# One Square for both token tiles of the q projection, and other places for sink copies, reciprocals and weight splits, in a hybrid decoder step

## The chip, the cores and the metric

The kernel runs on one core of a Trainium2 chip. TensorE (PE) multiplies and transposes, VectorE (DVE), ScalarE (ACT) and GpSimd (POOL) do the rest, and SyncE (SP) issues DMAs. The metric is the device time of the whole program in microseconds, the median of several runs. The times and the profile of the kernel before were shown ahead of the prediction; of the changed kernel its code and the order of its instructions, and no time.

## What is computed

One layer of a decoder, for a prompt of 2048 tokens and for 8 sample tokens. Inputs are normalised and modulated, one projection gives q, k, v and the gates, and two branches follow: sliding-window attention with normalised q and k and a sink in the softmax, and a gated linear recurrence. Gated projections merge both.

```
h = _rmsnorm(x, norm_g) * (1.0 + scale) + shift
z = h @ w_in
q, k, v, ga, xr, gr, ma, mr = jnp.split(z, offs, axis=-1)
q = _rmsnorm(q.reshape(B, T, N_HEADS, HEAD_DIM), q_g)
k = _rmsnorm(k.reshape(B, T, KV_HEADS, HEAD_DIM), k_g)
...
logits = jnp.einsum('bnqkgd,bnskd->bnkgqs', qb, kb) * ATT_SCALE
logits = jnp.where(valid, logits + _rel_bias(rel_table, dist), NEG)
p = softmax(concatenate([logits, sinks]))[..., :-1]
o = jnp.einsum('bnkgqs,bnskd->bnqkgd', p, vb)
ya = o * jax.nn.silu(ga)
...
merged = jax.nn.sigmoid(ma) * (ya @ w_pa) + jax.nn.sigmoid(mr) * (yr @ w_pr)
y = x + gate * (merged @ w_out)
```

D_MODEL is 1024, with 16 query heads and 4 key heads of 64, and a window of 128. The change lies in the prompt's attention, where q is projected and normalised.

## The kernel before, in words

All matrix products of float32 data are made of three: each operand is split into a high and a low part (`split_raw`: ACT copies the high part, DVE subtracts it from the raw data for the low part), and high x high, high x low and low x high are summed in PSUM. Weights arrive raw by DMA in tiles of 128x512 and are split on the chip; one such split is one CAST on ACT and one TENSOR_TENSOR on DVE.

The prompt is worked in two halves of 1024 tokens (s = 0, 1). Each half has an attention pass (`phase_attn`), which in the profile takes about 108 to 340 us and 1035 to 1258 us, and a long run of projections after it (`line`).

An attention pass loops over i = 0 to N + 1, with N = 16. Iteration i stands for q group u = i // 4 (four heads, 256 columns of w_in) and token block tp = i % 4 (two tiles t = 0, 1 of 128 tokens). It is a software pipeline of three steps: iteration i projects and normalises q of step i, does the scores and the softmax of step i-1, and the products with v of step i-2. The stages, by the names of the code:

- `gemm_a`, twice ("half 0" and "half 1", one for each token tile): 24 matmuls of 128x256 into columns 0:256 and 256:512 of one PSUM bank, `pg`. In the profile these are the rows `MATMUL pg<-B,S 128x256`.
- `stage_a1(ps, ss, t)` for each half: ACT squares the half (`ACTIVATE H<-pg 128x256`), DVE sums the squares of each head (`TENSOR_REDUCE M<-H 128x4`), and POOL takes mean, epsilon and the power -1/2 (`rstd_of`: `TENSOR_SCALAR M<-M`, `TENSOR_TENSOR M<-M,mhalf`).
- `stage_a2`: DVE multiplies q by that factor, once for each tile (`TENSOR_TENSOR B<-pg,M 128x256`).
- `stage_b1` of step i-1: PE transposes q (four matmuls `pt<-ident,B`, between half 0 and half 1), ACT and DVE make its high and low part (`ACTIVATE B<-pt,qg`, `SCALAR_TENSOR_TENSOR B<-pt,qg,B`).
- `stage_b2`: the scores, 64-row matmuls into `pq`, `pg` and `pt`. `stage_b0`: POOL copies the sinks into the last column of the softmax tile (`COPY B<-skn 128x4`). `stage_b3`, once for each tile: DVE masks and adds the bias (`COPY_PREDICATED`, then a custom reduction, named ISA in the order), ACT takes four exps.
- `stage_b4` of step i-2: DVE's RECIPROCAL of the sums, and POOL's product with it (`TENSOR_TENSOR B<-B,M 128x512`), once for each tile.
- `stage_c1` of step i-2: eight transposes of the softmax tiles (four for each tile), then "parts": for each tile an ACT copy (`COPY B<-pt`) and a DVE product with a mask (`TENSOR_TENSOR B<-pt,mcT`). `stage_c2`: 16 matmuls with v. `stage_c3` takes them out.
- `fill`: a gate projection's matmuls, in the first and last iterations; `slot(n)`: pieces of the following projections, in i = 13 to 16; in the second pass also the sample's own steps (`stage_s`, `samples_gemm`), small matmuls of 8 rows and their norm, in the iterations with tp > 0.
- `weights(n, end)`: takes the splits that are due, by a list of (place, end) pairs. The q weights of u = 1, 2, 3 are four splits each, due at places 3 to 6, 11 to 14 and 19 to 22, where place 2i stands for the first part of iteration i and 2i + 1 for its later part, and end = 0 or 1 for two spots in each. The last gate weights (called gKT here) are due at 31.

Every instruction of the pass goes through the wrapper `Pinned` (line 60 in all rows of the profile), which keeps program order: each engine runs its instructions in the order in which they are written, and waits at the first one that is not ready. So the order of the calls in the loop is the order on every engine. Tiles come from rings: `B` (`Tt`, 35 tiles of 128x512) and `H` (6 of 128x256).

Of the kernel before, what the change touches and what calls it, by code (L numbers as in the profile page):

```python
# [26 lines left out]
HD = 64  # L27
# [14 lines left out]
def tile_hybrid_step(ctx: ExitStack, tc: tile.TileContext, x_prompt, x_sample, cache_k, cache_v, state_conv,  # L42
# [63 lines left out]
    def H(shape, dt=F32):  # L106
        return hp.tile([P] + shape, dt, tag="H", name=nm("H"))
# [132 lines left out]
    def rstd_of(dst, ss, n, inv):  # L240
        G_.tensor_scalar(dst, ss, inv, EPS, op0=ALU.mult, op1=ALU.add)
        G_.tensor_tensor(dst, dst, mhalf[0:dst.shape[0], 0:n], op=ALU.pow)
# [315 lines left out]
    def phase_attn(s, hT, sa, kT, vt, chunks, line):  # L558

        ya, mbs, kcs = {}, {}, {}  # L560

        def stage_a1(ps, ss, t):
            sq = H([256])
            A.activation(sq, ps[:, t * 256:(t + 1) * 256], AF.Square)
            o = ss[:, 4 * t:4 * t + 4]
            V.tensor_reduce(o, sq.rearrange("p (h d) -> p h d", d=HD), op=ALU.add, axis=AX.X)
            rstd_of(o, o, 4, 1.0 / HD)

        def stage_a2(ps, ss):
            qn = Tt([2, 2, 2, HD])  # L570
# [243 lines left out]
        for i in range(N + 2):  # L814
            gsm_ready = len(gsm)

            def fill(n):
                nonlocal hdone
                while hdone < n:
                    evac = ga_half(hdone)  # L820
                    if evac:
                        evac()
                    hdone += 1

            def slot(n):
                if N - 3 <= i <= N:
                    line.emit(4 * (i - N - 1) + n)

            if 2 <= i:
                lt_[i - 2] = [stage_b4(*sm_[i - 2][0])]  # L830
            weights(2 * i, 0)
            if 2 <= i:
                lt_[i - 2].append(stage_b4(*sm_.pop(i - 2)[1]))
            if 1 <= i <= N:
                ub, tb = seq[i - 1]
                if tb == 0 and ub % 2 == 0:
                    mbs[ub // 2] = S([8, P])
                    ld.dma_start(mbs[ub // 2], Md[:, ub // 2 * 8:ub // 2 * 8 + 8])
            slot(0)
            if i < N:  # L840
                u, tp = seq[i]
                ps_[i], ss_[i] = PG(), M([8])
                gemm_a(ps_[i], wqs[u], hT, 2 * tp * P, 0)
                stage_a1(ps_[i], ss_[i], 0)
            elif i == N:
                fill(nh - 3)
            else:
                line.emit(0)
            if 1 <= i <= N:
                qk_[i - 1] = stage_b1(ub, tb, qn_.pop(i - 1))  # L850
            weights(2 * i, 1)
            slot(1)
            if i < N:
                if s == 1 and tp == 1:
                    next(smp[u])
                if pend:
                    next(pend.pop(0))
                gemm_a(ps_[i], wqs[u], hT, (2 * tp + 1) * P, 1)
                if pend:
                    next(pend.pop(0))  # L860
                if tp == 3:
                    drop(wqs.pop(u))
                if s == 1 and tp == 1:
                    next(smp[u])
                stage_a1(ps_[i], ss_[i], 1)
            elif i == N:
                fill(nh - 2)
            else:
                line.emit(1)
            weights(2 * i + 1, 0)  # L870
            if 2 <= i:
                t2 = seq[i - 2][1]
                c_[i - 2] = [stage_c1(2 * t2 + t, lt) for t, lt in enumerate(lt_.pop(i - 2))]
                c_[i - 2] = [fn() for fn in c_[i - 2]]
            slot(2)
            if i == N + 1:
                line.emit(2)
            if 1 <= i <= N:
                lps = stage_b2(ub, tb, *qk_.pop(i - 1))
                lts = [stage_b0(ub) for _ in range(2)]  # L880
            if 2 <= i:
                u2, t2 = seq[i - 2]
                po = stage_c2(u2, c_.pop(i - 2))
                if u2 == 3:
                    free(vt[1][t2])
            if 1 <= i <= N:
                sm_[i - 1] = [stage_b3(ub, 2 * tb, lps[0], lts[0])]
            if i < N:
                qn_[i] = stage_a2(ps_.pop(i), ss_.pop(i))
            if 2 <= i and u2 > 0:  # L890
                stage_c3(u2, t2, po)
            if 1 <= i <= N:
                sm_[i - 1].append(stage_b3(ub, 2 * tb + 1, lps[1], lts[1]))
                if ub % 2 and tb == 3:
                    free(mbs.pop(ub // 2), *kT[ub // 2])
            fill(want[i] if i < N else nh)
            if 2 <= i and u2 == 0:
                stage_c3(u2, t2, po)
            if 2 <= i and t2 == 3:
                for f in (2 * u2, 2 * u2 + 1):  # L900
                    st.dma_start(yad[s, f], ya[f])
                    free(ya.pop(f))
            weights(2 * i + 1, 1)
            if s == 1 and i < N and tp > 0:
                next(smp[u])
            if gsm and gsm_ready:
                next(gsm.pop(0))
            slot(3)
# [1236 lines left out]
```

## Time and profile before

| what | value |
| --- | --- |
| runs before, median | 1985.59 us (1983.94 to 1988.86, three runs) |
| the profiled execution | 1991.77 us, its span from first to last instruction 1990.1 us |
| mean granted clock of TensorE | 0.995 |
| busy PE, DVE, ACT, POOL | 97%, 69%, 50%, 21% of the span |
| instructions | 32504 |

A line of the costliest groups gives engine, operation, out<-in by the names of tiles, shape, count, then busy us in all and mean ns of one, then the idle time of the engine just ahead of these instructions and what ended most of it. A line of the timeline gives start in us from the span's start, duration in us, engine and operation, how many alike were merged, and in brackets the idle time ahead and its releaser. A row of the windows gives the stretch and its length, then the busy time of PE, of its weight loads (PEld), DVE, ACT and POOL, the granted clock (1.00 is full), and the share and GB/s of the DMA engines. A row of the waits reads: who waited <- for whom: us in all, times, longest.

### The profile page before, as it was taken

How to read it: one execution, taken by the hardware profiler on the slowest of the kernel's cores; microseconds unless marked ns; L12 is line 12 of the kernel's file. 1: busy time of each engine (PE TensorE's matmuls, PEld its weight loads, DVE VectorE, ACT ScalarE, POOL GpSimd, SP SyncE). 2: the span in 40 equal slices, each digit the busy share in tenths (PEclk: the TensorE clock that was granted, in tenths of full speed). 3: DMA queues.
4: the chain of work that ended last, by engine and by line, in shares of the span. 5: the costliest groups of instructions: out<-in, count | busy, mean ns of one | idle time of the engine just before them, and what ended most of it. 6: DMA issues, size and time to landing. Idle time of an engine off the chain costs nothing. (4 is left out here: it accounts for less than half of the span.)

```text
span 1990.1 us, 32504 instructions
## 1 busy us (share of the span) xinstructions
PE 1930.7 (97%) x11504; PEld 1571.9 (79%) x11504; DVE 1375.0 (69%) x2894; ACT 988.4 (50%) x2199; POOL 409.4 (21%) x540
## 2 busy tenths in 40 slices
PE   6899999999999999999999999999999999999999
PEld 4788887778888878887898888777887877777777
DVE  3447777766878885578744766677677879754965
ACT  4335555435665766514423555543465757542221
POOL 4113443000201112152012344310011111111600
PEclk9999999999999999999999999999999999999999
DMA  9520214552433457986622121445233334458673
GB/s 304 178 75 12 86 49 148 151 183 87 150 98 113 143 180 226 321 296 191 224 60 57 36 62 49 143 130 153 78 118 100 127 102 164 141 174 291 219 230 111
DMA packets 307688, 286.62 MB, mean 144 GB/s; under 512 B 57073, under 2 KB 224229, under 8 KB 307486
## 3 DMA queue, kind: packets, MB, share of 16 engines
q1 hardware_dynamic: 307398, 282.41, 45.3%
q8 instruction: 90, 1.47, 0.3%
q0 software_dynamic: 128, 2.15, 0.3%
q14 instruction: 72, 0.59, 0.1%
HBM read 200.69 MB, written 85.93 MB: 144 GB/s over the span
## 5 line engine op out<-in xcount | busy, mean ns | idle before, releaser
L60 PE MATMUL pg<-S,B 128*128 128x512 f32 (+1 forms) x4224 | 1003.8, 392 | 4.2 <-DVE B L60 3.8
L60 PEld LDWEIGHTS pg<-S,B 128*128 128x128 f32 (+1 forms) x4224 | 773.5, 188 | 189.5 <-issue 11.9
L60 DVE TENSOR_TENSOR B<-B,B 128x512 fp32r<-128x512 f32 (+1 forms) x732 | 537.8, 757 | 157.7 <-ACT B L60 147.9
L60 PE MATMUL pq<-S,B 128*128 128x512 f32 (+2 forms) x1920 | 411.0, 378 | 5.9 <-DVE B L60 5.7
L60 PEld LDWEIGHTS pq<-S,B 128*128 128x128 f32 (+1 forms) x1920 | 316.3, 187 | 84.1 <-DVE B L60 9.7
L60 POOL TENSOR_TENSOR B<-B,B 128x512 f32<-128x512 f32 x128 | 191.3, 1511 | 926.3 <-DVE B L60 518.3
L60 ACT CAST B<-B 128x512 fp32r<-128x512 f32 x468 | 280.3, 617 | 111.2 <-DVE B L60 72.1
L60 PE MATMUL pg<-B,S 128*128 128x256 f32 x1872 | 249.0, 289 | 17.6 <-ACT H L60 12.8
L60 PEld LDWEIGHTS pg<-B,S 128*128 128x128 f32 x1872 | 231.9, 192 | 36.6 <-ACT H L60 19.8
L60 ACT CAST S<-B 128x512 fp32r<-128x512 f32 x184 | 108.8, 620 | 95.8 <-DVE B L60 40.3
L60 DVE TENSOR_TENSOR S<-B,S 128x512 fp32r<-128x512 f32 x184 | 143.2, 808 | 14.8 <-ACT S L60 14.6
L60 ACT ACTIVATE B<-B 128x512 f32<-128x512 f32 (+1 forms) x150 | 93.1, 630 | 116.4 <-DVE B L60 108.7
L60 ACT ACTIVATE B<-B,M 128x129 f32<-128x129 f32 x260 | 102.6, 396 | 72.1 <-DVE M L60 53.4
L60 POOL TENSOR_TENSOR B<-B,M 128x512 f32<-128x512 f32 x64 | 70.4, 1121 | 170.4 <-DVE M L60 170.4
L60 DVE SCALAR_TENSOR_TENSOR B<-B,pg 128x512 f32<-128x512 f32 x78 | 53.1, 682 | 74.8 <-PE pg L60 67.0
L60 POOL TENSOR_TENSOR M<-M,mhalf 128x4 f32<-128x4 f32 (+3 forms) x102 | 96.3, 944 | 8.5
L60 DVE TENSOR_TENSOR B<-pq,B 128x512 f32<-128x512 f32 x96 | 65.9, 686 | 44.1 <-PE pq L60 37.9
L60 ACT COPY B<-pg 128x512 f32<-128x512 f32 x80 | 46.9, 586 | 90.1 <-PE pg L60 81.7
L60 DVE TENSOR_REDUCE M<-H 128x4 f32<-128x256 f32 (+1 forms) x85 | 35.1, 414 | 80.3 <-ACT H L60 79.0
L60 ACT COPY H<-pt 128x256 f32<-128x256 f32 (+1 forms) x47 | 15.6, 333 | 150.1 <-PE pt L60 150.1
L60 DVE SCALAR_TENSOR_TENSOR B<-B,VT,B 128x512 f32<-128x512 f32 x96 | 81.1, 845 | 2.3
L60 DVE SCALAR_TENSOR_TENSOR B<-B,B 128x512 f32<-128x512 f32 x106 | 72.0, 684 | 0.4 <-ACT B L60 0.2
(201 smaller groups left out, 1711.5 us busy)
## 6 DMA issues: line engine op xcount, KB each, us to landing
B<-in_w_in_dram SPq DMA_DIRECT2D x144, 256.0 KB
B<-in_w_in_dram SPq DMA_DIRECT2D x128, 128.0 KB
B<-yad SPq DMA_DIRECT2D x56, 256.0 KB
B<-hd SPq DMA_DIRECT2D x48, 256.0 KB
B<-in_w_out_dram SPq DMA_DIRECT2D x48, 256.0 KB
S<-in_w_ada_dram SPq DMA_DIRECT2D x32, 256.0 KB
S<-in_x_prompt_dram SPq DMA_DIRECT2D x16, 512.0 KB
hd<-B SPq DMA_DIRECT2D x32, 256.0 KB
```

Of the source, the lines that this page charges most:

```text
L60: ins = fn(*args, **kw)
```

## The change

`stage_a1` now squares the whole bank with one ACT instruction, after half 1, into a tile of the `B` ring. The reduction and the factor are a stage of their own, `stage_a3`: one TENSOR_REDUCE to 128x8 and one eight-wide `rstd_of`, behind the parts of c1. The sinks' copies of `stage_b0` stand ahead of these parts. `weights` is called once in an iteration, between the transposes of b1 and half 1. `slot(2)` stands behind c2. The two `stage_b4` are written as one list.

```diff
@@ -559,12 +559,17 @@
 
         ya, mbs, kcs = {}, {}, {}
 
-        def stage_a1(ps, ss, t):
-            sq = H([256])
-            A.activation(sq, ps[:, t * 256:(t + 1) * 256], AF.Square)
-            o = ss[:, 4 * t:4 * t + 4]
-            V.tensor_reduce(o, sq.rearrange("p (h d) -> p h d", d=HD), op=ALU.add, axis=AX.X)
-            rstd_of(o, o, 4, 1.0 / HD)
+        def stage_a1(ps):
+            sq = Tt([512])
+            A.activation(sq, ps, AF.Square)
+            return sq
+
+        def stage_a3(sq):
+            ss = M([8])
+            V.tensor_reduce(ss, sq.rearrange("p (h d) -> p h d", d=HD), op=ALU.add, axis=AX.X)
+            free(sq)
+            rstd_of(ss, ss, 8, 1.0 / HD)
+            return ss
 
         def stage_a2(ps, ss):
             qn = Tt([2, 2, 2, HD])
@@ -827,10 +832,7 @@
                     line.emit(4 * (i - N - 1) + n)
 
             if 2 <= i:
-                lt_[i - 2] = [stage_b4(*sm_[i - 2][0])]
-            weights(2 * i, 0)
-            if 2 <= i:
-                lt_[i - 2].append(stage_b4(*sm_.pop(i - 2)[1]))
+                lt_[i - 2] = [stage_b4(*x) for x in sm_.pop(i - 2)]
             if 1 <= i <= N:
                 ub, tb = seq[i - 1]
                 if tb == 0 and ub % 2 == 0:
@@ -839,16 +841,15 @@
             slot(0)
             if i < N:
                 u, tp = seq[i]
-                ps_[i], ss_[i] = PG(), M([8])
+                ps_[i] = PG()
                 gemm_a(ps_[i], wqs[u], hT, 2 * tp * P, 0)
-                stage_a1(ps_[i], ss_[i], 0)
             elif i == N:
                 fill(nh - 3)
             else:
                 line.emit(0)
             if 1 <= i <= N:
                 qk_[i - 1] = stage_b1(ub, tb, qn_.pop(i - 1))
-            weights(2 * i, 1)
+            weights(2 * i + 1, 1)
             slot(1)
             if i < N:
                 if s == 1 and tp == 1:
@@ -862,27 +863,30 @@
                     drop(wqs.pop(u))
                 if s == 1 and tp == 1:
                     next(smp[u])
-                stage_a1(ps_[i], ss_[i], 1)
+                sq = stage_a1(ps_[i])
             elif i == N:
                 fill(nh - 2)
             else:
                 line.emit(1)
-            weights(2 * i + 1, 0)
             if 2 <= i:
                 t2 = seq[i - 2][1]
                 c_[i - 2] = [stage_c1(2 * t2 + t, lt) for t, lt in enumerate(lt_.pop(i - 2))]
+            if 1 <= i <= N:
+                lts = [stage_b0(ub) for _ in range(2)]
+            if 2 <= i:
                 c_[i - 2] = [fn() for fn in c_[i - 2]]
-            slot(2)
+            if i < N:
+                ss_[i] = stage_a3(sq)
             if i == N + 1:
                 line.emit(2)
             if 1 <= i <= N:
                 lps = stage_b2(ub, tb, *qk_.pop(i - 1))
-                lts = [stage_b0(ub) for _ in range(2)]
             if 2 <= i:
                 u2, t2 = seq[i - 2]
                 po = stage_c2(u2, c_.pop(i - 2))
                 if u2 == 3:
                     free(vt[1][t2])
+            slot(2)
             if 1 <= i <= N:
                 sm_[i - 1] = [stage_b3(ub, 2 * tb, lps[0], lts[0])]
             if i < N:
@@ -900,7 +904,6 @@
                 for f in (2 * u2, 2 * u2 + 1):
                     st.dma_start(yad[s, f], ya[f])
                     free(ya.pop(f))
-            weights(2 * i + 1, 1)
             if s == 1 and i < N and tp > 0:
                 next(smp[u])
             if gsm and gsm_ready:
```

Three places show how the order of instructions moves. The first is on PE, iteration i=6 of the first pass, at the step from half 0 over the transposes of b1 to half 1 (`pg_2417` before and `pg_2387` now are the projection's bank, `pt_...` the transposes' bank). Before:

```order
L60 MATMUL pg_2417<-B_1959,S_869 128x256
L60 MATMUL pg_2417<-B_1958,S_869 128x256
L60 MATMUL pt_2448<-ident_81,B_2390 128x128 [waits DVE_49,PE_49]
L60 MATMUL pt_2448<-ident_81,B_2390 128x128
L60 MATMUL pt_2448<-ident_81,B_2390 128x128 [waits DVE_49]
L60 MATMUL pt_2448<-ident_81,B_2390 128x128
L60 MATMUL pg_2417<-B_1711,S_337 128x256 [waits Activation_49]
L60 MATMUL pg_2417<-B_1712,S_337 128x256
```

and now:

```order
L60 MATMUL pg_2387<-B_1938,S_869 128x256
L60 MATMUL pg_2387<-B_1937,S_869 128x256
L60 MATMUL pt_2412<-ident_81,B_2364 128x128 [waits DVE_49,PE_49]
L60 MATMUL pt_2412<-ident_81,B_2364 128x128
L60 MATMUL pt_2412<-ident_81,B_2364 128x128 [waits DVE_49]
L60 MATMUL pt_2412<-ident_81,B_2364 128x128
L60 MATMUL pg_2387<-B_1583,S_337 128x256
L60 MATMUL pg_2387<-B_1584,S_337 128x256
```

The same instructions stand in the same order; the first matmul of half 1 no longer waits for ACT.

The second place is on ACT in the same iteration, from the last exps of the iteration ahead to the first copy of c1's parts (CAST is the split's part; `pt_2448` and `pt_2412` are b1's transposes, `pt_2501` and `pt_2466` those of c1). Before:

```order
L60 ACTIVATE B_2367,M_2400<-B_2367,M_2393 128x129 [waits DVE_49] x3
L60 CAST B_2409<-B_1763 128x512 [waits DMAHW1_49,DMAHW0_49,Activation_49]
L60 ACTIVATE H_2443<-pg_2417 128x256 [waits PE_49]
L60 ACTIVATE B_2453<-pt_2448,qg_944 128x512 [waits PE_49]
L60 CAST B_2457<-B_1766 128x512 [waits DMAHW3_49,DMAHW2_49]
L60 ACTIVATE H_2491<-pg_2417 128x256 [waits PE_49]
L60 COPY B_2509<-pt_2501 128x512 [waits PE_49,Activation_49]
```

and now:

```order
L60 ACTIVATE B_2301,M_2374<-B_2301,M_2367 128x129 [waits DVE_49] x3
L60 ACTIVATE B_2417<-pt_2412,qg_944 128x512 [waits PE_49,Activation_49]
L60 CAST B_2421<-B_1750 128x512 [waits DMAHW3_49,DMAHW2_49,Activation_49]
L60 CAST B_2431<-B_1941 128x512 [waits DMAHW5_49,DMAHW4_49,Activation_49]
L60 ACTIVATE B_2459<-pg_2387 128x512 [waits PE_49,Activation_49]
L60 COPY B_2478<-pt_2466 128x512 [waits PE_49]
```

The first half's Square is gone and the second covers 512 columns; both CASTs stand between the high part of q and that Square, where before one stood ahead of the first Square.

The third place is DVE in the same iteration, from b4's reciprocals to the first mask copy of b3 (`mcT` marks c1's products). Before:

```order
L60 TENSOR_TENSOR B_2410<-B_1763,B_2409 128x512 [waits DMAHW1_49,DMAHW0_49,Activation_49]
L60 RECIPROCAL M_2385<-M_2385 128x4
L60 RECIPROCAL M_2400<-M_2400 128x4
L60 TENSOR_REDUCE M_2418<-H_2443 128x4 [waits Activation_49]
L60 SCALAR_TENSOR_TENSOR B_2454<-pt_2448,qg_944,B_2453 128x512 [waits Activation_49]
L60 TENSOR_TENSOR B_2458<-B_1766,B_2457 128x512 [waits DMAHW3_49,DMAHW2_49,Activation_49]
L60 TENSOR_REDUCE M_2418<-H_2491 128x4 [waits Activation_49]
L60 TENSOR_TENSOR B_2506<-pt_2496,mcT_90 128x512 [waits PE_49]
L60 TENSOR_TENSOR B_2508<-pt_2501,mcT_90 128x512 [waits Activation_49]
L60 COPY_PREDICATED pq_2512<-maskf_88,pq_2512 128x2x128 [waits PE_49]
```

and now:

```order
L60 RECIPROCAL M_2359<-M_2359 128x4 [waits Activation_49]
L60 RECIPROCAL M_2374<-M_2374 128x4 [waits Activation_49]
L60 SCALAR_TENSOR_TENSOR B_2418<-pt_2412,qg_944,B_2417 128x512 [waits Activation_49]
L60 TENSOR_TENSOR B_2422<-B_1750,B_2421 128x512 [waits DMAHW3_49,DMAHW2_49,Activation_49]
L60 TENSOR_TENSOR B_2432<-B_1941,B_2431 128x512 [waits DMAHW5_49,DMAHW4_49,Activation_49]
L60 TENSOR_TENSOR B_2475<-pt_2461,mcT_90 128x512 [waits PE_49]
L60 TENSOR_TENSOR B_2477<-pt_2466,mcT_90 128x512 [waits Activation_49]
L60 TENSOR_REDUCE M_2481<-B_2459 128x8
L60 COPY_PREDICATED pq_2485<-maskf_88,pq_2485 128x2x128 [waits PE_49]
```

The reciprocals stand ahead of both subtractions, and the one wide reduction stands between c1's products and the mask copy, where before each reduction stood ahead of them.

## The prediction

> **What bounds the kernel now.** I read the page first, then the windows by stage, then the waits of PE in the two attention passes, and last the timeline around single waits.
>
> From the page, busy time of PE, and the group of the q projection (busy us, mean ns, then idle time ahead of it and its main releaser):
>
> ```profile
> PE 1930.7 (97%) x11504; PEld 1571.9 (79%) x11504; DVE 1375.0 (69%) x2894; ACT 988.4 (50%) x2199; POOL 409.4 (21%) x540
> L60 PE MATMUL pg<-B,S 128*128 128x256 f32 x1872 | 249.0, 289 | 17.6 <-ACT H L60 12.8
> ```
>
> The windows of the first attention pass, the long projections after it, and the second pass (length, then busy time of each engine):
>
> ```profile
> 108.00:340.00 232.00, 220.88 (x1797) 191.12 (x1797) 153.54 (x516) 116.99 (x396) 87.26 (x136) 0.99 0.23 69
> 360.00:1035.00 675.00, 672.25 (x3121) 545.16 (x3120) 485.78 (x756) 344.98 (x608) 99.83 (x94) 1.00 0.56 178
> 1035.00:1255.00 220.00, 213.59 (x1852) 188.56 (x1852) 142.61 (x486) 116.61 (x387) 83.40 (x136) 1.00 0.17 52
> ```
>
> PE sets the time everywhere. The projections have 2.75 us without PE in 675, so nothing is to be had there. The attention passes have 11.1 and 6.4 us. The waits of PE in them (total, times, longest; first pass, then two rows of the second):
>
> ```profile
> PE pg L60 <- ACT H L60: 7.9, 13, 1.8
> ...
> PE pg L60 <- ACT H L60: 4.9, 6, 1.0
> PE pt L60 <- POOL B L60: 1.2, 4, 0.3
> ```
>
> So 12.8 us, in 19 waits, come from one place: the first matmul of half 1 waits for the Square of half 0, because both halves write one PSUM bank. PE rows of three cases, a long wait, the shortest kind, and a succession without any:
>
> ```profile
> 200.03 3.10 PE L60 MATMUL pg<-B,S 128*128 128x256 f32 x24 [0.93 <-ACT H L60]
> ...
> 165.27 0.60 PE L60 MATMUL pt<-ident,B 128*128 128x128 f32 x4
> 165.91 0.51 PE L60 MATMUL pg<-B,S 128*128 128x256 f32 x2
> ...
> 225.43 0.40 PE L60 MATMUL pg<-B,S 128*128 128x256 f32 x2
> 225.67 1.04 PE L60 MATMUL pt<-ident,B 128*128 128x128 f32 x8
> ```
>
> Matmuls in succession overlap: the group at 225.67 starts 0.16 before the one ahead ends (225.83). I take 0.14 as the mean, so that a listed wait costs its idle time plus 0.14: 9.7 us in the first pass (7.9 + 13 x 0.14), 5.7 in the second (4.9 + 6 x 0.14). At 165.91 the half comes 0.04 after the transposes' end, too short to be listed, yet about 0.19 late against an overlapped start. I count three of these in the first pass and six in the second: 0.6 and 1.2 us. Together **10.3** and **6.9** us. Four iterations of the second pass lose nothing, since sample matmuls stand between the transposes and half 1.
>
> **The change part by part.**
>
> *One Square for both halves.* By the order, no half 1 waits for ACT any more; its bank's next reader comes behind it. Hence up to 17.2 us go. The long waits are those with a weight split ahead of the Square:
>
> ```profile
> 199.09 0.60 ACT L60 CAST B<-B 128x512 fp32r<-128x512 f32 x1
> ...
> 199.60 0.37 ACT L60 ACTIVATE H<-pg 128x256 f32<-128x256 f32 x1
> ```
>
> The Square that releases PE at 200.03 stood behind this CAST. The splits now stand behind half 0's transposes, where PE has the 3.1 us of half 1 to run, and at i=15 of the first pass they no longer delay DVE's c1 products, which cost PE this wait in c2, **0.4**:
>
> ```profile
> 307.97 0.65 PE L60 MATMUL pt<-B,S 128*64 128x256 f32 x4 [0.41 <-DVE B L60]
> ```
>
> *The clock.* At i=0 of the first pass:
>
> ```profile
> 116.76 4.64 PE L60 MATMUL pg<-B,S 128*128 128x256 f32 x24 [1.84 <-ACT H L60]
> ...
> 118.00:120.00 2.00, 2.00 (x11) 2.00 (x11) 0.35 (x1) 0.22 (x1) 0.93 (x1) 0.50 0.01 4
> 120.00:122.00 2.00, 2.00 (x13) 1.91 (x12) 0.00 (x0) 0.35 (x1) 0.00 (x0) 0.73 0.00 0
> ```
>
> Behind the idle 1.84 us the granted clock is 0.50, and 24 matmuls take 4.64 instead of 3.10 us. Without the wait I count these **1.5** us saved too; bounds 0 (the clock falls anyway) and 2. The Trainium skill, "TensorE: Matmul & The Clock Gate", section "What's actually happening", has the clock halved after an idle window of about 3.4 us. The trace disagrees as far as it goes: 1.84 us were followed by 0.50. Were the page's length to decide, the drop would have another cause and the sum would be 1.5 us less.
>
> *What the path through ACT, DVE and POOL pays.* One regular iteration (all engines, first pass):
>
> ```profile
> 225.87 0.38 ACT L60 ACTIVATE H<-pg 128x256 f32<-128x256 f32 x1 [2.61 <-PE pg L60]
> 226.28 0.42 DVE L60 TENSOR_REDUCE M<-H 128x4 f32<-128x256 f32 x1 [2.24 <-ACT H L60]
> ...
> 226.79 0.19 POOL L60 TENSOR_SCALAR M<-M 128x4 f32<-128x4 f32 x1 [1.45 <-DVE M L60]
> 226.92 1.29 DVE L60 TENSOR_TENSOR B<-pt,mcT 128x512 f32<-128x512 f32 x2 [0.22 <-ACT B L60]
> 227.07 1.01 POOL L60 TENSOR_TENSOR M<-M,mhalf 128x4 f32<-128x4 f32 x1
> ...
> 228.13 0.42 DVE L60 COPY_PREDICATED pq<-maskf,pq 128x256 f32<-128x256 int32 x1
> ...
> 230.14 0.75 DVE L60 TENSOR_TENSOR B<-pg,M 128x256 f32<-128x256 f32 x2
> ...
> 233.07 2.04 POOL L60 TENSOR_TENSOR B<-B,M 128x512 f32<-128x512 f32 x2 [4.72 <-DVE M L60]
> ...
> 236.81 0.38 PE L60 MATMUL pt<-ident,B 128*128 128x128 f32 x2
> ```
>
> and the nearest rows for the wider instructions (an ACT activation of 512, a DVE reduction of 36, POOL's power of one column):
>
> ```profile
> L60 ACT ACTIVATE B<-pg 128x512 f32<-128x512 f32 x44 | 26.1, 593 | 47.0 <-PE pg L60 47.0
> L60 DVE TENSOR_REDUCE modT<-pt 128x9 f32<-128x36 f32 x24 | 4.0, 189 | 16.8 <-PE pt L60 16.8
> L60 POOL TENSOR_TENSOR M<-M,mhalf 128x1 f32<-128x1 f32 x16 | 9.4, 589 | 1.3
> ```
>
> The Square takes 0.59 instead of 0.38, which moves the copies behind it and the c1 products by 0.21. The reduction, now of 512 and between the products and the mask copy of 228.13 instead of under ACT's copies, is 0.65 to 0.83: a line through 36 elements in 189 ns and 256 in 420 gives 0.69, twice the old one 0.84. I take 0.69, less 0.05 of overlap. So everything from 228.13 on comes **0.85** us later in its iteration (bounds 0.8 to 1.1), down to the softmax products of POOL. POOL's power of 8 columns lies between 1.0 (as of 4) and 2.0 (twice); the line through 589 and 1010 gives 1.6, and ending at about 229.0 + 0.25 + 1.6 = 230.9, it just meets the norm at 230.14 + 0.85 = 231.0. At 2.0 the norm waits 0.4 more. The two sink copies of about 0.16 each now run ahead, in POOL's wait for DVE, and free the exps no later.
>
> What waits for this: the products end at 235.11, and the c1 transposes of the second tile follow those of 236.81 by two pairs, at about 237.3. With half 1's delay of 0.33 gone, 237.0: slack 1.85 us, of which 0.85 to 1.5 is used. Regular iterations stay with PE.
>
> *Three iterations of the second pass* (i=6, 10, 14) have none of this slack, since the sample's norm stands ahead of POOL's products:
>
> ```profile
> 1141.49 3.09 PE L60 MATMUL pg<-B,S 128*128 128x256 f32 x24 [1.03 <-ACT H L60]
> ...
> 1237.90 3.10 PE L60 MATMUL pg<-B,S 128*128 128x256 f32 x24 [0.52 <-ACT H L60]
> ...
> 1140.89 0.69 DVE L60 TENSOR_TENSOR B<-B,B 128x512 fp32r<-128x512 f32 x1 [0.52 <-ACT B L60]
> 1141.50 0.40 DVE L60 TENSOR_REDUCE M<-H 8x4 f32<-8x256 f32 x1
> ...
> 1142.95 0.97 DVE L60 TENSOR_TENSOR B<-B,B 128x512 fp32r<-128x512 f32 x1
> ...
> 1143.24 2.58 POOL L60 TENSOR_TENSOR B<-B,M 128x512 f32<-128x512 f32 x2
> ...
> 1239.36 2.03 POOL L60 TENSOR_TENSOR B<-B,M 128x512 f32<-128x512 f32 x2
> ...
> 1241.44 0.20 PEld L60 LDWEIGHTS pt<-ident,B 128*128 128x128 f32 x2 [0.25 <-POOL B L60]
> ```
>
> The first two rows are the first and last of the three waits for the Square: 1.17, 1.17 and 0.66 with the overlap, 3.0 us, which PE now spends waiting for POOL instead. On top, POOL ends later: at i=14 by 0.85. At i=6 and 10 the split that stood ahead of the sample's reduction (1140.89) is gone, CAST and all, worth 0.6, but two splits now run beside the products instead of one. One split beside them made 2.03 into 2.58 (1143.24); I take half of such a step, 0.27, for the second, so 0.85 - 0.6 + 0.27 = 0.5 each. In sum 3.0 + 0.85 + 1.0 = **4.9** us given back. The Trainium skill, "SBUF — State Buffer", section "Who interferes with whom", speaks against this placing: an operation of VectorE with two SBUF inputs and one of GpSimd that reads SBUF block each other fully, one after the other. Here they slow each other by 0.55 us, less than the 0.69 of a split. By the page, two splits would add 1.4 to the 2.03, which is rival (e).
>
> *At nothing:* 32 Squares, 32 reductions and 64 POOL instructions fewer (none on PE's path but as counted); the reciprocals' list, since by the order nothing passed between them but a split that does not exist there; SP, whose order is unchanged; the last iterations, where slot(2) behind c2 holds loads (0 to 0.4 us gain).
>
> **Sum.** 10.3 + 0.4 + 1.5 in the first pass, 6.9 - 4.9 = 2.0 in the second: 14.2 us off the profiled execution's 1991.77 (span 1990.1), which leaves 1977.6. The median of the runs shown is 1985.59, 6.2 below that execution; the waits are counts of one program order, so I take the same 14.2 off it: **1971** us.
>
> **The rivals.**
> (a) *Full recovery*: POOL's three iterations hurt nothing, as their b3 finds DVE free earlier. 10.3 + 6.9 + 0.4 + 1.5 and the 1.2 of PE's POOL waits and 0.4 at the end: 20.7, so 1965. Against it: the b3 chain gets later, not earlier.
> (b) *POOL late in all the second pass* (power at 2.0, reduction at 0.84, so 1.5 used there, and the sample's instructions in most iterations): the second pass gains nothing or loses 1. 12.2 - 1 = 11, so 1974.5. A delay of 0.5 in the first pass's ten split and edge iterations too makes it 1980.
> (c) *No change*: the wait for the Square is replaced one for one by c1 transposes waiting for the softmax products in both passes; within 6 us of before, 1980 to 1986. It needs 0.5 us over the slack in each of some 24 iterations (24 x 0.5 = 12).
> (d) *Slower*: the same mechanism past its break-even. Each microsecond by which the chain's shift passes 1.85 costs 24 us; the 14.2 are gone at a shift of 2.45, and 0.3% are lost at 2.7: 1992. My upper bounds (0.21 + 0.84 + 0.4 of waiting for the power) reach 1.5, so a further 1.2 us would have to appear in DVE's or POOL's queue.
> (e) *DVE's splits and POOL's products exclude each other*: two splits of 0.69 stand wholly ahead of or inside the products, so 2.03 + 1.38 = 3.41 instead of my 2.58 + 0.27 = 2.85, 0.56 more in i=6 and 10 of the second pass: 1.1 us, so 1972. Against it: 2.58 with one split is under 2.03 + 0.69 = 2.72, though not by much. This is the page's rule above.
> (f) *The wait stays*: against it the order, where no first matmul of a half 1 names ACT. I give it nothing.
>
> **How the numbers follow.** Forecast 0.40 (1968 to 1974), (e) 0.15, (a) 0.12, (b) 0.17, (c) 0.11, (d) 0.05. A measurement of this kernel tells 0.3%, 6 us, from no change, so faster means under 1979.6: forecast, (e), (a) and nearly all of (b), 0.83; same 0.12; slower 0.05. The range leaves out (d), the upper part of (c), and what lies under full recovery: 1963 to 1980.
>
> **What would show it.** In the changed profile: no row of PE pg waiting for ACT at half 1; clock 1.00 in the window that answers to 118 to 122; the wide reduction near 0.69, the wide power near 1.6, the Square 0.59; the mask copy 0.85 later after c1's first transpose; PE's wait for POOL B a few us in the second pass, none in the first. Wrong would be: waits of c1's transposes for POOL in ordinary iterations, or b1's transposes waiting for a norm that waits for the power.

## The result and the profile after

The changed kernel takes 1971.31 us (median of four runs, 1966.93 to 1974.05) against 1984.94 before, on the same chip: a ratio of 0.9926 with a 95% interval of 0.9902 to 0.9949, or 10 to 19 us less. The prediction said 1971, 14.2 us less.

From the page of the changed kernel: busy time of PE, and the group of the q projection (columns as before):

```profile
PE 1918.4 (98%) x11504; PEld 1566.4 (80%) x11504; DVE 1377.1 (70%) x2862; ACT 983.3 (50%) x2167; POOL 393.5 (20%) x476
L60 PE MATMUL pg<-B,S 128*128 128x256 f32 x1872 | 244.7, 286 | 0.6 <-ACT S L60 0.6
```

Its 17.6 us of idle time ahead, 12.8 of them for ACT's Square, are 0.6. The waits of PE in the first pass up to its last iteration, then in the second (total, times, longest):

```profile
PE pt L60 <- DVE B L60: 1.4, 1, 1.4
...
PE pt L60 <- POOL B L60: 5.9, 6, 1.5
PE pt L60 <- ACT S L60: 2.0, 1, 2.0
PE pt L60 <- DVE M L60: 0.4, 1, 0.4
```

So the first pass has one listed wait left, at its very end, and the second has exchanged its 4.9 us for the Square against 4.7 us more for POOL.

Whole times scatter by up to 11 us for one kernel, so the parts are read from the profiles. PE runs the same 11504 matmuls in all kernels here. The table gives the us between the starts of matmuls 1, 501, 2501, 5501, 7751 and 11504: the opening, the first attention pass, the projections, the second pass, the rest. Each pass is counted with some 10 to 18 us that lead into it and some 28 to 43 us of the projections behind it. The letters are those of the experiments below.

| kernel | opening | first pass | projections | second pass | rest |
| --- | --- | --- | --- | --- | --- |
| before | 86.7 | 278.5 | 656.6 | 276.8 | 684.0 |
| changed | 81.1 | 262.3 | 656.8 | 273.9 | 683.8 |
| changed again (f1) | 80.9 | 262.3 | 656.2 | 273.9 | 685.1 |
| Square only (e1) | 82.7 | 269.7 | 656.5 | 274.0 | 683.5 |
| splits only (e2) | 86.1 | 273.5 | 657.2 | 272.6 | 684.8 |
| splits back (e3) | 82.5 | 270.2 | 656.5 | 280.3 | 683.9 |
| reciprocals first (f3) | 86.3 | 263.5 | 657.0 | 273.7 | 686.0 |
| more on POOL (f4) | 85.7 | 283.2 | 656.2 | 273.8 | 684.2 |
| reduction first (g1) | 81.6 | 262.7 | 656.2 | 270.6 | 684.3 |
| slot(2) as before (g2) | 84.9 | 262.6 | 656.8 | 273.9 | 684.0 |
| sample's norm moved (e4) | 85.4 | 262.2 | 656.2 | 268.2 | 684.4 |
| the same again (f2) | 81.7 | 262.3 | 656.4 | 268.2 | 683.9 |
| and fill first (g3) | 85.7 | 262.3 | 656.4 | 264.8 | 684.3 |

The passes repeat to 0.1 us (changed and f1, e4 and f2). In the two profiled executions the change took 16.2 us from the first pass and 2.9 from the second, 19.1 together; the other 5.7 of the difference of their spans (1990.1 and 1965.2) lie in the opening, which takes 80.9 to 86.7 us whatever the kernel, and 81.7 and 85.4 us for one and the same (f2 and e4).

The regular iteration of the changed kernel, first pass (to be held against the rows from 225.67 on in the prediction; c1's first transposes are at 211.59):

```profile
211.59 1.03 PE L60 MATMUL pt<-ident,B 128*128 128x128 f32 x8
211.79 0.60 ACT L60 ACTIVATE B<-pg 128x512 f32<-128x512 f32 x1 [1.66 <-PE pg L60]
214.10 0.68 DVE L60 TENSOR_REDUCE M<-B 128x8 f32<-128x512 f32 x1
214.69 0.42 DVE L60 COPY_PREDICATED pq<-maskf,pq 128x256 f32<-128x256 int32 x1
215.15 1.64 POOL L60 TENSOR_TENSOR M<-M,mhalf 128x8 f32<-128x8 f32 x1
216.82 0.75 DVE L60 TENSOR_TENSOR B<-pg,M 128x256 f32<-128x256 f32 x2
218.96 0.60 PE L60 MATMUL pt<-ident,B 128*128 128x128 f32 x4
219.32 3.08 PE L60 MATMUL pg<-B,S 128*128 128x256 f32 x24
219.75 2.04 POOL L60 TENSOR_TENSOR B<-B,M 128x512 f32<-128x512 f32 x2 [2.97 <-DVE M L60]
222.24 1.03 PE L60 MATMUL pt<-ident,B 128*128 128x128 f32 x8
```

Half 1 follows b1's transposes without a wait (218.96, 219.32). The mask copy comes 3.10 us after c1's first transposes, where it came 2.46 after them before: 0.64 later. POOL's products end at 221.79, the second tile's transposes are due at about 222.24 + 0.5: 0.95 us to spare.

### The profile page after: what moved, and what is told of

It is laid out like the page before. It is cut to its first block, busy times and chain, and to the rows that moved or that the text cites. A ratio compares the mean times of both kernels' runs of the same rounds, so it can differ in the third digit from the quotient of the medians.

```text
span 1965.2 us, 32362 instructions
## 1 busy us (share of the span) xinstructions
PE 1918.4 (98%) x11504; PEld 1566.4 (80%) x11504; DVE 1377.1 (70%) x2862; ACT 983.3 (50%) x2167; POOL 393.5 (20%) x476
## 5 line engine op out<-in xcount | busy, mean ns | idle before, releaser
L60 PE MATMUL pg<-B,S 128*128 128x256 f32 x1872 | 244.7, 286 | 0.6 <-ACT S L60 0.6
L60 ACT COPY B<-pg 128x512 f32<-128x512 f32 x80 | 46.9, 586 | 89.4 <-PE pg L60 81.1
L60 ACT ACTIVATE B<-pg 128x512 f32<-128x512 f32 x76 | 45.2, 595 | 84.9 <-PE pg L60 84.9
L60 POOL TENSOR_TENSOR M<-M,mhalf 128x8 f32<-128x8 f32 (+4 forms) x70 | 83.4, 1192 | 5.8
L60 DVE TENSOR_TENSOR B<-pt,mcT 128x512 f32<-128x512 f32 x64 | 41.7, 686 | 45.5 <-ACT B L60 43.7
```

Source lines behind the costliest of these rows:

```text
L60: ins = fn(*args, **kw)
```

## The experiments

**e1, the Square alone.** The wide Square and the reduction, behind half 1; all else as before.

```diff
-                stage_a1(ps_[i], ss_[i], 0)
...
-                stage_a1(ps_[i], ss_[i], 1)
+                ss_[i] = stage_a3(stage_a1(ps_[i]))
```

> The wide Square and the wide reduction alone, behind half 1 and ahead of c1's parts; splits, sink copies, reciprocals and slot(2) stay where they were. Measured by the PE time between the same matmuls in the profiles: the first attention pass of the changed kernel is 16.2 us shorter than before, the second 2.9. Theory (the bank's Square is the whole wait, the places of the splits matter only for POOL): no half 1 waits for ACT, 15 to 16 us less in the first pass, 2.5 to 4 in the second (one split instead of two beside POOL's products), so 1966 to 1973 us. Rival (the splits' places make the long waits, the Square the short ones): 10 us or less in the first pass, and about 1977.

1976.58 us, a ratio of 0.9933 (0.9914 to 0.9951). The first pass is 8.8 us shorter than before, not 16.2. No half 1 waits for ACT, as the theory said, and yet the rival's numbers came. What PE waits for in the first pass, from 100 to 300 us:

```profile
PE pt L60 <- POOL B L60: 3.2, 4, 0.8
PE pt L60 <- DVE B L60: 0.8, 1, 0.8
```

c1's transposes wait for the softmax products at i=6, 7, 10 and 11, four of the iterations with splits. My theory of what the splits' places do had a hole: with the Square's wait gone, they do matter on PE's path in the first pass.

**e2, the splits' place alone.** One call of `weights`, each half with its own Square.

```diff
-            weights(2 * i, 0)
...
-            weights(2 * i, 1)
+            weights(2 * i + 1, 1)
...
-            weights(2 * i + 1, 0)
...
-            weights(2 * i + 1, 1)
```

> The splits at their one new place, nothing else; each half keeps its own Square. Theory: the four waits of 1.1 to 1.2 us at i=6, 7, 10, 11 of the first pass fall to 0.35 each (3.2 us less), the one of 2.0 at i=0 falls under 0.5 and the clock stays at 1.00 behind it (together 3 us), c2 at i=15 gets its 0.4: 6 to 7 us in the first pass; in the second 1 to 2. So about 1977. Rival (the splits' places carry half of the gain or more): 9 us or more over both passes, 1975 or less. Both leave the waits for ACT of about 0.2 to 0.35 in every iteration.

1982.42 us, 0.9954 (0.9937 to 0.9971). First pass 5.0 us shorter, second 4.2. The waits for the Square in the first pass, 7.9 us before, are

```profile
PE pg L60 <- ACT H L60: 4.9, 13, 0.8
```

so the short ones stay, in 13 of the 16 iterations, as both sides said. The theory was a little high for the first pass (6 to 7) and far too low for the second (1 to 2); 9.2 us over both is the rival's figure. The whole time of 1982.42 meets neither side's 1977 or 1975, with an opening of 86.1 us in the profiled execution. Together the two parts alone make 13.8 us in the first pass, the change 16.2. Of the 2.4 us between, 1.9 lie at the pass's end, whose long wait (2.56 us before) both parts leave in place and the change shortens to 1.43; up to matmul 2251 they add up, 14.0 us together and 14.4 for the change. In the second pass the splits' place alone is worth more than the whole change (272.6 and 273.9), so what the change does beside it costs 1.3 there.

**e3, the splits back.** The changed kernel with `weights` at the four old places.

> The changed kernel with the splits put back to their four old places. Theory: as the wide Square alone within 1 us in either pass, since the sink copies, the reciprocals, slot(2) and the place of the reduction cost and bring nothing on PE's path; POOL's products at i=6 and 10 of the second pass then run beside one split, and PE's waits for POOL there fall from 2.3 us each to about 1.3. Rival (the places of the small parts matter): it differs from the wide Square alone by over 2 us in a pass.

1983.08 us, 0.9969 (0.9957 to 0.9981). The first pass is within 0.5 us of e1, but only in sum: up to matmul 2251 it is 2.3 us longer, with 5.2 us of waits for POOL instead of 3.2, and its end is 1.8 shorter. The second is 280.3, 6.4 us over e1 and 3.5 over the kernel before. About 2 us of that are two stretches of halved clock, behind waits of 2.31 and 2.20 us (see f3). Even so the theory is refuted in both passes: where products are late, the places of the small parts count. Iteration 6 of the first pass in e3, by DVE, POOL and PE:

```profile
190.04 0.61 ACT L60 CAST B<-B 128x512 fp32r<-128x512 f32 x1
190.68 0.69 DVE L60 TENSOR_TENSOR B<-B,B 128x512 fp32r<-128x512 f32 x1 [0.52 <-ACT B L60]
191.28 0.24 DVE L60 RECIPROCAL M<-M 128x4 f32<-128x4 f32 x2
191.60 2.48 POOL L60 TENSOR_TENSOR B<-B,M 128x512 f32<-128x512 f32 x2 [4.92 <-DVE M L60]
192.70 0.66 PE L60 MATMUL pt<-ident,B 128*128 128x128 f32 x4 [0.45 <-POOL B L60]
194.14 0.66 PE L60 MATMUL pt<-ident,B 128*128 128x128 f32 x4 [0.79 <-POOL B L60]
```

The last exp ends and the CAST begins at 190.04. DVE idles for that CAST, subtracts, and only then takes the reciprocals, 1.24 us after the exps' end; POOL's products start behind them, and PE waits for both tiles.

**f3, only the reciprocals ahead of the splits.** To test that reading: the four old places, but no split ahead of the two reciprocals. At least as many subtractions run beside POOL's products.

```diff
             if 2 <= i:
                 lt_[i - 2] = [stage_b4(*x) for x in sm_.pop(i - 2)]
+            weights(2 * i, 0)
...
-            weights(2 * i + 1, 1)
+            weights(2 * i, 1)
...
+            weights(2 * i + 1, 0)
```

> The changed kernel with the splits at their old places but for one thing: none stands ahead of the two reciprocals (the split of an iteration's end and that between the two reciprocals come just behind both). As many subtractions run beside POOL's products as with the old places, or more. Theory (with the old places the products were late because their reciprocals queued on DVE behind a subtraction that itself waited for a CAST behind the last exp): PE's waits for POOL in the first pass fall from 5.2 us to under 1.5, and the pass takes 262 to 264.5 us, not 270.2; the second 272 to 276, not 280.3. Rival (subtractions beside the products slow them, wherever the reciprocals stand): 3 us or more of these waits stay in the first pass.

The first pass takes 263.5 us, the second 273.7. PE's waits for POOL in the first, 5.2 us in e3, are

```profile
PE pt L60 <- POOL B L60: 0.2, 1, 0.2
```

So of the 7.9 us by which e3's first pass is longer than the changed kernel's, 6.7 come from the reciprocals' place in DVE's queue. Subtractions beside the products matter little in comparison: at i=6 the two products take 2.49 us instead of 2.04, and PE waits 0.2 for them, the one wait that is left.

In the second pass e3 and f3 differ by 6.6 us, and not all of that is the reciprocals' place. Both wait 2.20 us for ACT at the pass's end, but e3's clock is halved behind that wait and f3's is not, which makes 1.6 us (the window of 2 us that begins 2 us behind the end of the wait, e3 and then f3):

```profile
1250.63:1252.63 2.00, 2.00 (x6) 1.52 (x6) 0.89 (x2) 0.73 (x3) 2.00 (x2) 0.50 0.00 0
...
1243.32:1245.32 2.00, 2.00 (x12) 1.66 (x12) 0.89 (x2) 0.73 (x3) 2.00 (x2) 1.00 0.00 0
```

Another halved clock in e3, behind 2.31 us of waiting for POOL at i=10, makes some 0.5. The other 4.5 come from the reciprocals' place, 2.3 each at i=6 and 10.

**f4, more on POOL.** A further power of 4 columns between each reciprocal and its product, first pass only.

```diff
             V.reciprocal(sm, sm)
+            if s == 0:
+                G_.tensor_tensor(M([4]), sm, mhalf[:, 0:4], op=ALU.pow)
```

> The changed kernel with one more power of 4 columns on POOL (1.0 us, its result not used) ahead of each softmax product of the first pass, behind its reciprocal. Theory (the products end 0.95 us before PE needs them in a regular iteration, so 2.0 us more make the second 1.1 us late): the first pass gets 11 to 18 us longer, with PE's waits for POOL in nearly every iteration. Rival (POOL has 2 us and more to spare in the first pass): under 4 us longer. The second pass stays at 273.9.

The first pass is 20.9 us longer, beyond the theory's 11 to 18. PE's waits there:

```profile
PE pt L60 <- POOL B L60: 16.6, 13, 1.8
```

An iteration of the regular kind, from one step's first score matmul to the next, takes 11.62 us instead of 10.68, 0.94 longer; so 2.0 us more overshoot a margin of 1.1, against 0.95 from the timeline. Other iterations have less to spare: with tp = 2 one takes 12.06 instead of 10.24, and six others, splits among them, grow by 1.4 to 2.0. These, and one halved clock behind a wait of 1.76 us, make the excess over the forecast. The rival is refuted: in its regular iterations the changed kernel stands about 1 us from being bound by POOL in the first pass.

**e4 and f2, the sample's norm.** In the changed kernel, the norm of the sample's q is issued behind POOL's products of the next iteration, not ahead of them.

```diff
                 lt_[i - 2] = [stage_b4(*x) for x in sm_.pop(i - 2)]
+            if s == 1 and i < N and seq[i][1] == 2:
+                next(smp[seq[i][0]])
...
-            if s == 1 and i < N and tp > 0:
+            if s == 1 and i < N and tp > 1:
```

> The changed kernel with the sample's norm (ACT Square 8x256, DVE reduction, two POOL instructions) at the start of the next iteration, behind POOL's softmax products instead of ahead of them. Theory (those POOL instructions ahead of the products are what is late in i=6, 10, 14 of the second pass): PE's 5.9 us of waits for POOL in that pass fall to 2 or less, the pass is 4 to 6 us shorter than the changed kernel's, about 1967. Rival (two splits that block the products are what is late): the waits at i=6 and 10 stay at over half of their 4.6 us, and the pass gets at most 3 us shorter.

> The kernel with the sample's norm behind POOL's products once more. Theory: 5 to 7 us under the changed kernel, or 0.3%; second pass 266.7 us without, 268.2 us with a drop of the clock at its end; about 0.987 of the kernel before. Rival (the gain of its first runs was the state of the clock): within 2 us of the changed kernel.

1964.5 us, 0.9868 (0.9852 to 0.9884), and 1964.18, 0.988 (0.9868 to 0.9893): 6.8 and 8.6 us under the changed kernel's two medians (1971.31 here, 1972.74 in f1); the second pass is 5.7 shorter, with a halved clock at its end that the changed kernel does not have. All six waits for POOL are gone: PE's waits in e4's second pass are

```profile
PE pt L60 <- ACT S L60: 2.0, 1, 2.0
PE pt L60 <- DVE M L60: 0.4, 1, 0.4
```

Iterations 6, 10 and 14 take 10.66, 10.68 and 10.65 us, where they took 13.01, 13.01 and 11.66 before and 13.41, 13.42 and 12.43 in the changed kernel. So the norm ahead of the products made them late: at i=6 they begin 0.28 us behind the last exp, where they began 2.17 behind it in the changed kernel. The run does not by itself exclude the rival's splits, since the earlier products are half over when the first subtraction begins, and escape it (1.04 us each, where the two took 3.02). But at i=14, where no split runs, PE waited 1.3 us for the products in the changed kernel, so the norm suffices; and in f3's first pass the slower products cost PE 0.2 us in all. In i=6 and 10 both added to the lateness, 1.9 us the norm and 1.0 the splits.

**f1, the changed kernel again.**

> The changed kernel once more, with more rounds. Theory: the two attention passes take 262.3 and 273.9 us again within 0.3 us, if no wait of about 2 us is followed by a halved clock; the whole is about 0.7 to 0.9% under the kernel before, and what runs differ in lies ahead of the first pass and in such drops of the clock. Rival (the passes themselves vary by some us): a pass differs by over 1 us without such a drop.

1972.74 us (1966.54 to 1977.82), 0.9929 (0.991 to 0.9949). The passes are the same to 0.1 us in the profiled execution. The six runs fall into 1966.5, 1967.6 and 1969.5 us with mean granted clocks of 0.999, 0.997 and 0.997, and 1976.0, 1977.1 and 1977.8 with 0.995, 0.994 and 0.994. A clock lower by 0.003 over 1966 us is about 6 us of the 9 between the groups, so stretches of halved clock are likely most of it; where these lie in runs without a profile can't be seen. The opening alone varies by 5.8 us over the thirteen profiles.

**g1, the reduction first.** The wide reduction and its factor ahead of c1's parts.

```diff
-                sq = stage_a1(ps_[i])
+                ss_[i] = stage_a3(stage_a1(ps_[i]))
...
-            if i < N:
-                ss_[i] = stage_a3(sq)
```

> The changed kernel with the wide reduction and its factor ahead of c1's parts, as the second reduction stood before the change. Theory (the reduction's place delays b3 by some 0.6 us, which only iterations feel whose products are late): first pass as before this edit, 262.3 us within 0.5; second 1 to 2 us shorter than 273.9, since i=6, 10 and 14 get up to 0.6 each. Rival (the place matters on PE's path everywhere): the first pass changes by over 2 us.

First pass 262.7 us, second 270.6, 3.3 shorter than the changed kernel's: i=6, 10 and 14 take 0.6 less each, as expected; that the whole is more than the 1 to 2 expected comes from i=4 (0.57: the wait for DVE there is gone) and i=16 (0.73). The place that the change gave the reduction brings 0.4 us in the first pass and costs 3.3 in the second.

**g2, slot(2) as before in the first pass.** To explain the shorter end of the first pass (below).

> The changed kernel with slot(2) ahead of b2 again in the first pass. Theory (the changed kernel's shorter wait at the end of the first pass, 1.43 us where it was 2.56, comes from slot(2), and the full clock behind it from the wait being short): the wait at the last c2 is 2.5 us again, the clock is halved behind it, and the first pass takes 264 us, not 262.3. Rival (the end is shorter because DVE and POOL have less in front of them there): 262.3 within 0.5, with a wait of about 1.4.

262.6 us, with the last c2's wait at 1.43: the rival's numbers came, and slot(2) has nothing to do with it. The rival's reason was not tested by itself.

**g3, the fill first.** e4, with 12 gate matmuls ahead of slot(0) at i=16.

```diff
-            slot(0)
+            if i != N:
+                slot(0)
...
             elif i == N:
                 fill(nh - 3)
+                slot(0)
```

> The kernel with the sample's norm behind POOL's products, and at i=16 the gate projection's 12 matmuls ahead of slot(0), whose sample matmuls wait 2.0 us for ACT in the second pass. Theory: these matmuls fill the wait, so no wait of over 1.2 us stays in the second pass and the clock stays at 1.00: 264.5 to 266.5 us in place of 268.2, the first pass within 0.5 of 262.3; 2 to 4 us under the kernel without this edit, about 1961. Rival (the wait moves to the next transposes, which need ACT too): 268 us again.

The wait of 2.0 us is gone and the second pass takes 264.8 us, 3.4 less than e4's. The median is 1961.94 us, 0.9874 (0.9856 to 0.9892), the lowest here; against e4 and f2 the intervals of the ratios don't tell them apart (e4's 0.9868 is even lower), the passes do.

## Why the prediction was right, point by point

*The wait for the Square: right.* The rows are gone. Its size was a little low: unhindered, half 1 starts 0.10 us nearer to the transposes than I allowed, so an unhindered succession saves 0.24 and not 0.14 over the listed idle time, and by the starts of the same matmuls in the two profiles the 17.2 us were 19.8 (11.9 and 7.9).

*The splits "behind half 0's transposes": right in effect, priced by the wrong reason.* I counted what they free on ACT, ahead of the Square. e1 and f3 show the other half: with the Square's wait gone, the old places would have made POOL's products late through DVE's queue, and cost 6.7 us in the first pass. The wait of 0.4 us in the c2 of i=15 is gone, as forecast; with the old places (e1, e3, f3) it stays, at 0.7 to 0.8.

*The path through ACT, DVE and POOL: right in mechanism, the shift mis-sized.* The steps, from the rows above and these groups of the changed kernel:

```profile
L60 ACT ACTIVATE B<-pg 128x512 f32<-128x512 f32 x76 | 45.2, 595 | 84.9 <-PE pg L60 84.9
L60 DVE TENSOR_REDUCE M<-B 128x8 f32<-128x512 f32 x32 | 21.6, 676 | 5.0 <-ACT B L60 5.0
L60 POOL TENSOR_TENSOR M<-M,mhalf 128x8 f32<-128x8 f32 x32 | 52.4, 1638 | 2.7
```

Square 0.595 (taken 0.59), reduction 0.676 (0.69), power 1.638 (1.6), shift of the mask copy 0.64 (0.85, bounds 0.8 to 1.1), margin left 0.95 to 1.1 (1.0). The straight lines through two neighbouring sizes were good. The shift lies under its bounds because the wider Square delayed c1's copies by 0.06 us and not 0.21: they begin 0.69 us behind the transposes, where they began 0.63 behind them. That the margin still came out is partly luck: each regular step also became 0.46 shorter, by the overlap above, where I had taken off 0.33.

*Three iterations of the second pass: right.* Forecast 0.5, 0.5 and 0.85 us longer than before, measured 0.40, 0.41 and 0.77. In these three c1's transposes start 4.9 us later against the matmuls ahead of them than before, the forecast's figure. Not in the forecast were 0.55 us at i=4, where PE now waits for DVE, and 0.60 at i=16, where it waits 2.03 instead of 1.43 for ACT; gains of some 1.0 spread over other iterations make up for them, so the 2.9 for the pass are what 7.9 less 4.9 leave, in part by chance. Iteration 6 of the changed kernel's second pass:

```profile
1118.52 0.19 POOL L60 TENSOR_SCALAR M<-M 8x4 f32<-8x4 f32 x1 [4.28 <-DVE M L60]
1118.79 1.00 POOL L60 TENSOR_TENSOR M<-M,mhalf 8x4 f32<-8x4 f32 x1
1119.26 2.63 DVE L60 TENSOR_TENSOR B<-B,B 128x512 fp32r<-128x512 f32 x2
1119.76 3.02 POOL L60 TENSOR_TENSOR B<-B,M 128x512 f32<-128x512 f32 x2
...
1121.39 0.66 PE L60 MATMUL pt<-ident,B 128*128 128x128 f32 x4 [1.52 <-POOL B L60]
...
1122.84 0.65 PE L60 MATMUL pt<-ident,B 128*128 128x128 f32 x4 [0.79 <-POOL B L60]
```

The price of the second split rested on a misread row. That one split made 2.58 us of 2.03 was taken as a slowing by less than the split's own 0.69; but its subtraction began at 1142.95, 0.29 ahead of the products, so the three took 2.87 us together, more than 0.69 and 2.03. Measured, the two splits made 3.02 us of the products, between the forecast's 2.85 and rival (e)'s 3.41, since the first 0.50 of the subtractions ran under POOL's power, ahead of the products.

*The clock, 1.5 us: it came* (the clock is 1.00 from 108.95 to 112.95, behind the start of half 1 at i=0), *but not as a property of the kernel* (last section).

*The end of the first pass, "0 to 0.4": mis-sized.* It gave some 2 us: the stretch from matmul 2251 to 2501 is 1.84 us shorter. The wait is 1.13 shorter and the halved clock behind it, about 1.5 us, is gone; 0.8 are lost again in the projections behind. The last instructions of DVE and POOL there, before and in the changed kernel:

```profile
335.70 2.57 DVE L60 TENSOR_TENSOR B<-B,B 128x512 f32<-128x512 f32 x2
336.46 1.26 POOL L60 TENSOR_TENSOR B<-B,B 128x512 f32<-128x512 f32 x1 [1.23 <-DVE B L60]
```

```profile
315.67 1.46 DVE L60 TENSOR_TENSOR B<-B,B 128x512 f32<-128x512 f32 x2
...
316.48 3.02 POOL L60 TENSOR_TENSOR B<-B,B 128x512 f32<-128x512 f32 x2 [1.29 <-PE pt L60]
```

Before, a POOL addition of the projections began 0.01 us ahead of DVE's second, which then took 1.80 us instead of 0.69 and held up the last c1 product; PE waited 2.56 us for it, and the clock was halved behind that. In the changed kernel POOL's begins 0.04 behind DVE's second: DVE's takes 0.69, POOL's 1.79 instead of 1.26, PE waits 1.43, and the clock stays. Why POOL starts later there (its releaser is PE, no longer DVE) is open. e3 and f3 show the short wait too, e1 and e2 the long one; e3 differs from e1 by the places of slot(2), of the reduction and of the sinks' copies, and g2 and g1 keep the short wait with the first or the second of them put back, so the sinks' copies are the likeliest suspect, which no run tests. The forecast's list of rows leaves this wait out, though it is a third of the 7.9 us that it lists for the Square.

*The rivals.* (a) fell with the 4.9 us given back; (b) was right of three iterations only, as forecast; (c) and (d) need what f4 had to add, more than 1 us on POOL in every iteration. (e) was nearer than the forecast in its reason, DVE and POOL in turns (last section), and its extra 0.56 us for each of i=6 and 10 did not come. (f) fell with the rows of the wait.

*The sum.* 14.2 us forecast; 14.7 and 14.1 by the two ratios, each give or take 4 to 5; 19.1 by the passes of one profiled execution each. The last holds two halved clocks of the kernel before, about 3 us, which another execution need not have. That the total was met so closely is luck. The passes gained more than forecast, by 2.6 us of overlap, 1.8 at the end and some 0.5 more, while the 1.5 of the clock need not come; runs without a profile show less of it, most likely because their openings and clocks vary by several us. The ratio's interval, 10 to 19 us, would have held other sums as well. What bears the forecast out is the parts, but for the sizes named here.

## What to carry to other kernels

An engine that waits on a shared PSUM bank is freed by doing the bank's reader once, behind its last writer; but look at once at what else stood behind that wait: here DVE's order of a reciprocal and a subtraction, harmless while PE waited, would have taken 6.7 of the 16.2 us of the first pass. Put what feeds the slowest side engine (here the reciprocals) ahead of everything in its producer's queue that nobody waits for. When an engine has a margin of 1 us in all iterations but three, the three are worth their own edit: it was the cheapest 5.7 us here.

## What the runs showed of the hardware

**The clock behind a wait.** The same wait in the second pass, with the same matmuls behind it, in the changed kernel and in e4 (PE rows, and the window of 4 us from the end of the wait):

```profile
1234.67 0.64 PE L60 MATMUL pt<-B,hsF 128*32 128x128 f32 x16 [2.03 <-ACT S L60]
1235.25 3.07 PE L60 MATMUL pg<-S,B 128*128 128x512 f32 x12
...
1234.67:1238.67 4.00, 4.00 (x33) 3.20 (x34) 2.65 (x13) 2.27 (x9) 2.11 (x2) 1.00 0.00 0
```

```profile
1231.13 0.65 PE L60 MATMUL pt<-B,hsF 128*32 128x128 f32 x16 [2.02 <-ACT S L60]
1231.70 4.61 PE L60 MATMUL pg<-S,B 128*128 128x512 f32 x12
...
1231.13:1235.13 4.00, 4.00 (x26) 3.09 (x27) 2.65 (x13) 2.27 (x9) 2.12 (x2) 0.68 0.00 0
```

2.03 us without PE left the clock at full speed, 2.02 us were followed by half speed, which cost 1.54 us. The halved stretch lasts 3.4 us in each of these cases. Over the thirteen profiles, behind the opening: of the waits up to 1.75 us one was followed by a halved clock (1.28 us, in the k and v stage of g2, where others precede it), of the twenty from 1.76 to 2.31 us eight were, and all four from 2.56 us on were. So a saving by "no halved clock" is a matter of chance for waits of this length, and my 1.5 us were in truth between 0 and 1.5. The Trainium skill, "TensorE: Matmul & The Clock Gate", section "What's actually happening", calls the activity window of about 3.4 us free-running, so that where it lies is a matter of when the work comes; this agrees with one wait giving either, while the length at which the clock falls here is shorter than the page's.

**DVE and POOL.** Two splits' subtractions and POOL's two products, begun 0.5 us apart, take from 1119.26 to 1122.78: 3.5 us, the sum of 1.4 and 2.03 undisturbed. So they run in turns, not side by side, at both engines' cost: the subtractions take 1.18 and 1.52 us, where one takes 0.69 alone. The Trainium skill, "SBUF — State Buffer", section "Who interferes with whom", says that an operation of VectorE with two SBUF inputs contends with one of GpSimd that reads SBUF, and that the one that comes second blocks fully. The trace agrees in the sum, and at the end of the first pass in the order too, where the second to begin, POOL or DVE, took the other's time on top (1.79 and 1.80 us). It does not agree for the first subtraction here, which was 0.50 us under way when the product began and still took 1.18. That all this cost PE only 0.4 us an iteration comes of the smaller shift: 0.64, less 0.6 for the split that is gone, and 0.44 for the longer products (3.02 instead of 2.58) make 0.48.
